# Where a split weight's remainder lies modulo 256 bytes: five wider buffers, each a pool of its own

## The chip, the cores and the metric

The kernel runs on one core of a Trainium2 chip. The metric is device time in microseconds (us) of one execution; lower is better. Three runs of the kernel before took 2660.53, 2660.72 and 2661.61 us, so its median is 2660.72 us. The engines are named as the profile names them: PE is the matrix engine (TensorE; PEld is its loading of weights), DVE is VectorE, ACT is ScalarE, POOL is GpSimd, SP is SyncE, which here issues most of the transfers.

## The reference

A decoder trunk of two layers over 256 positions of width 2048, all in float32:

```python
for i in range(DEPTH):                      # DEPTH = 2
    h = rms_norm(x, attn_norm[i])
    if i % 2 == 0:
        x = x + mla_mixer(h, ...)           # low-rank q and kv (rank 512), 16 heads, causal
    else:
        x = x + dilated_mixer(h, ...)       # 3 groups of windows (128,1), (512,4), (2048,16), 16 heads
    h = rms_norm(x, ffn_norm[i])
    x = x + conv_ffn(h, ...)                # up to 2 x 5632, causal convolution of width 3, silu gate, down
return rms_norm(x, final_norm)
```

Nearly all of the work is products of the 256 positions with weights that are read once: `dil_w_in` (2048 x 18432), `ffn_w_up` (2 x 2048 x 11264), `ffn_w_down` (2 x 5632 x 2048), the latent projections and the two output projections.

## The kernel before

**Split products.** Each float32 operand is split in two parts that PE multiplies in float32r form: a high part (`wh` of a weight, the first half of an activation tile) and the remainder (`wl`, the second half). ACT copies a piece of 1024 columns from the weights' ring `w` into `wh` (rounding it), DVE subtracts it from `w` and writes `wl`. A product is then high x high, high x low and low x high.

**Three ways to use a split weight.**
- A *unit* (`proj`, L142): the weight is the stationary operand and the activation `xs` or `a` the moving one. Matmuls with `wh` have 512 columns (high and low half of the activation together), those with `wl` 256 (the high half alone). All the wh matmuls of a unit come first and then all the wl ones, in the next unit the other way round (`runs`), so that up to 32 alike stand in a row. Projections of the dilated layer, up, down and output projections are units.
- *V* of the dilated layer (`load_tok2`, `proj_tok2`, L171 to L173): the activation is stationary, the weight moving, 512 columns. Three matmuls in turn: high with `wh`, low with `wh`, high with `wl`. V is done once for two pairs of heads and each of three groups, in four quarters.
- *Groups of seven products* in the feed-forward layers: four blocks of the up projection by Strassen's way, seven products in place of eight. `seven_ahead` (L957 to L959) uses sums of weights that were made earlier in HBM, `seven_here` (L1027 to L1029) makes them in SBUF for itself. The matmuls are of V's form: high with `wh`, low with `wh`, high with `wl`, weights moving. They are dealt out in portions of 6 or 12 matmuls between units (`slots`), after a unit's last matmul and with a wh run next.

The latent layer multiplies the normed latents `sqh` and `skvh` (256 columns, moving, or stationary for its V) with pieces of `wqb` and `wkvb` in `project` (through `mm3`, L109 to L111).

**Buffers.** Five buffers of 4096 bytes per partition for `wh` (pool `wsp`) and five for `wl` (pool `wspl`), each taken by whichever piece comes next as soon as one is free. Pools lie one behind the other. The residual stream, the activations `xs` and `a`, and `wh` all lie at one remainder modulo 256 bytes, since every pool between them takes a multiple of 256. Before `wspl` a tile `apart` of 64 bytes is put, so that all five `wl` buffers lie 64 bytes further, modulo 256. Behind them come `tab`, `work` (lo, sum and the like) and `small` (acc, sq, ms, rcol and small columns), also 64 bytes further, and then the weights' ring, where the remainder is that of `wh` again (the small pool is 192 bytes over a multiple of 256).

**Order.** Each engine runs its instructions in the order of the program. A unit first loads and splits its weights (`load`), then the matmuls follow, then a step or a portion of a group, then the evacuation of the unit before it. In the output projections (`out_proj`) and in the last down projection of a layer (`down` with `lastly`) two or three loads run ahead, and their products stop short of the last heads or blocks, which aren't ready; the rest of these products (`since`) follows later.

Of the kernel before, what the change touches and what calls it, by code (L numbers as in the profile page):

```python
# [18 lines left out]
F32 = mybir.dt.float32  # L19
# [14 lines left out]
RC = RANK // P  # L34
HEADS = 16
WS = 1024
NG = 3
GROUPS = ((128, 1), (512, 4), (2048, 16))
FFN = 5632
# [18 lines left out]
def trunk_kernel(tc, x_d, pos_d, gain_d, conv_d, const_d, mask_d, wqa_d, wkva_d, wqb_d, wkvb_d, wo_d,  # L58
                 win_d, dwo_d, wup_d, wdn_d, out_d):
    nc = tc.nc  # L60
    with ExitStack() as ctx:
# [1 line left out]
        resid = ctx.enter_context(tc.tile_pool(name="resid", bufs=1))  # L63
        wsp = ctx.enter_context(tc.tile_pool(name="wsp", bufs=5))
        act = ctx.enter_context(tc.tile_pool(name="act", bufs=16))
        apart = ctx.enter_context(tc.tile_pool(name="apart", bufs=1)).tile([P, 16], F32, name="apart", tag="apart")
        wspl = ctx.enter_context(tc.tile_pool(name="wspl", bufs=5))
        tab = ctx.enter_context(tc.tile_pool(name="tab", bufs=1))
        work = ctx.enter_context(tc.tile_pool(name="work", bufs=4))
        small = ctx.enter_context(tc.tile_pool(name="small", bufs=4))  # L70
# [5 lines left out]


        ring = {}

        def load(src, n, tok=0):  # L80

            some_ahead()
            wide = ring["wide"]
            w = []
            for a in range(0, n, wide):
                m = min(n - a, wide)
                t = ring["pool"].tile([P, wide], F32, name="w", tag="w")
                nc.sync.dma_start(t[:, :m], src[:, a:a + m])
                w += [t[:, c:c + min(m - c, WS)] for c in range(0, m, WS)]
            parts = []  # L90
            for i, w in enumerate(w):
                m = w.shape[-1]
                wh = wsp.tile([P, WS], F32R, name="wh", tag="wh")
                wl = wspl.tile([P, WS], F32R, name="wl", tag="wl")
                if i * WS < tok:
                    state["split"] = nc.scalar.activation(wh[:, :m], w, AF.Copy)  # L96
                    nc.vector.tensor_sub(wl[:, :m], w, wh[:, :m].bitcast(F32))  # L97
                else:
                    for h, t in enumerate((wh, wl)):
                        src2 = w[:, h * WS // 2:(h + 1) * WS // 2].rearrange("p (k c) -> p k c", c=T)  # L100
                        t4 = t.rearrange("p (k s c) -> p k s c", s=2, c=T)
                        nc.scalar.activation(t4[:, :, 0, :], src2, AF.Copy)
                        nc.vector.tensor_sub(t4[:, :, 1, :], src2, t4[:, :, 0, :].bitcast(F32))
                parts.append((wh, wl))
            return parts
# [40 lines left out]
        def load_tok2(srcs, q):  # L146


            some_ahead()
            w = ring["pool"].tile([P, D], F32, name="w", tag="w")  # L150
            for i, src in enumerate(srcs):
                nc.sync.dma_start(w[:, i * WS:(i + 1) * WS], src[q // 2][:, q % 2 * WS:(q % 2 + 1) * WS])
            w4 = w.rearrange("p (i k c) -> p i k c", i=2, c=T)
            parts = []
            for h in range(2):
                wh = wsp.tile([P, WS], F32R, name="wh", tag="wh")
                wl = wspl.tile([P, WS], F32R, name="wl", tag="wl")
                wh4, wl4 = (t.rearrange("p (k i c) -> p i k c", i=2, c=T) for t in (wh, wl))
                src = w4[:, :, 2 * h:2 * h + 2, :]
                nc.scalar.activation(wh4, src, AF.Copy)  # L160
                nc.vector.tensor_sub(wl4, src, wh4.bitcast(F32))  # L161
                parts += [(wh[:, ts(k, 512)], wl[:, ts(k, 512)]) for k in range(2)]
            return parts
# [138 lines left out]
        xs = [None] * KC  # L302
        dil_rope = []

        def squares(src, i, name, adder=nc.vector):
            if i == 0:
                acc = small.tile([P, T], F32, name="acc", tag="acc", bufs=2)
                state[name] = acc
                nc.scalar.activation(acc, src, AF.Square)
            else:  # L310
                sq = small.tile([P, T], F32, name="sq", tag="sq", bufs=1)
                nc.scalar.activation(sq, src, AF.Square)
                adder.tensor_add(state[name], state[name], sq)
# [41 lines left out]

        def rstd_x(paired=False, last=None):
            ps = sumsq("x", paired, last)
            ms = small.tile([P, 2], F32, name="ms", tag="ms", bufs=2)
            nc.vector.tensor_scalar(ms, ps, 1.0 / D, EPS, op0=ALU.mult, op1=ALU.add)
            r = small.tile([P, 2], F32, name="rcol", tag="rcol", bufs=2)  # L360
            nc.gpsimd.tensor_tensor(r, ms, negh, op=ALU.pow)
            return r

        def rstd_rank(name, rcol):

            ps = sumsq(name)
            r2 = small.tile([P, 2], F32, name="r2", tag="r2", bufs=1)
            nc.vector.tensor_mul(r2, rcol, rcol)
            ms = small.tile([P, 2], F32, name="ms", tag="ms", bufs=2)
            nc.vector.scalar_tensor_tensor(ms, ps, 1.0 / RANK, r2, op0=ALU.mult, op1=ALU.mult)  # L370
            nc.vector.tensor_scalar(ms, ms, EPS, None, op0=ALU.add)
            s = small.tile([P, 2], F32, name="s2", tag="s2", bufs=2)
            nc.gpsimd.tensor_tensor(s, ms, negh, op=ALU.pow)
            nc.vector.tensor_mul(s, s, rcol)
            return s
# [123 lines left out]
        def mla():  # L499
            mask = lat.tile([P, P + T], F32, name="mask")  # L500

            def keep_rank(name, b, res, ps):
                t = work.tile([P, T], F32, name="lo", tag="lo", bufs=2)
                nc.scalar.activation(t, ps[:, T:], AF.Copy)
                a = lat.tile([P, T], F32, name=f"rank{b}", tag=f"rank{b}")
                nc.vector.tensor_add(a, ps[:, :T], t)
                squares(a, b, name)
                res.append(a)

            st = {}  # L510
# [38 lines left out]
            for k in range(KC):  # L549
# [2 lines left out]
                if k % 4 == 0:  # L552
                    w = ring["pool"].tile([P, D], F32, name="w", tag="w")
                if k % 2 == 0:
                    wh = wsp.tile([P, WS], F32R, name="wh", tag="wh")
                    wl = wspl.tile([P, WS], F32R, name="wl", tag="wl")
                c = k % 2 * RANK
                if k % n == 0:
                    a = k % 4 * RANK
# [58 lines left out]


            def project(j):  # L620
                wq = load(wqb_d[j], 3 * RC * P, tok=D)
                wkv = load(wkvb_d[j], 4 * RC * P, tok=WS)
                h = {}

                def keep_q(e, ps):
# [225 lines left out]
        def ffn(layer, goff, ready):  # L851
# [9 lines left out]

            def col():
                rb["r"] = rstd_x()
                rb["n"] = small.tile([P, 2], F32, name="ms", tag="ms", bufs=2)
                nc.vector.tensor_scalar(rb["n"], rb["r"], -1.0, None, op0=ALU.mult)

            def wide():
# [44 lines left out]
            def seven_ahead(fb0):  # L912
# [6 lines left out]
                def product(i, q):  # L919
# [25 lines left out]
                        w4 = w4.rearrange("p f k c -> p k f c")  # L945
                        tiles += [w4[:, k:k + 2] for k in range(0, n, 2)]
                    for h, w5 in enumerate(tiles):
                        wh = wsp.tile([P, WS], F32R, name="wh", tag="wh")
                        wl = wspl.tile([P, WS], F32R, name="wl", tag="wl")
                        as4 = lambda t: t.rearrange("p (k f c) -> p k f c", k=2, f=4)  # L950
                        nc.scalar.activation(as4(wh), w5, AF.Copy)  # L951
                        nc.vector.tensor_sub(as4(wl), w5, as4(wh).bitcast(F32))  # L952
                        for k in range(2):
                            kk = 4 * q + 2 * h + k
                            xh, xl = stationary(name, kk)
                            bh, bl = wh[:, ts(k, HALF)], wl[:, ts(k, HALF)]
                            nc.tensor.matmul(ps[i], xh, bh, start=(kk == 0), stop=False)  # L957
                            nc.tensor.matmul(ps[i], xl, bh, start=False, stop=False)  # L958
                            nc.tensor.matmul(ps[i], xh, bl, start=False, stop=(kk == KC // 2 - 1))  # L959
# [58 lines left out]
            def seven_here(fb0):  # L1018
# [9 lines left out]
                    nc.tensor.matmul(ps[i], xl, wh, start=False, stop=False)  # L1028
                    nc.tensor.matmul(ps[i], xh, wl, start=False, stop=(kk == KC // 2 - 1))  # L1029

                def pair():
                    wh = wsp.tile([P, WS], F32R, name="wh", tag="wh")
                    wl = wspl.tile([P, WS], F32R, name="wl", tag="wl")
                    return wh, wl

                raw = {}

                def first(kk):
# [10 lines left out]
                    as4 = lambda t: t.rearrange("p (i f c) -> p i f c", i=2, f=4)  # L1049
                    t13 = fpool.tile([P, 2 * HALF], F32, name="t13", tag="t13")  # L1050
                    t24 = fpool.tile([P, 2 * HALF], F32, name="t24", tag="t24")
                    (bh, bl), (ch, cl) = pieces = [pair() for _ in range(2)]

                    nc.scalar.activation(as4(bh), w5[:, 0], AF.Copy)
                    nc.vector.tensor_add(as4(t13), w5[:, 1], w5[:, :, 0])
# [5 lines left out]

                def second(kk):
                    w5, t1, t4, t24 = raw[0]
                    dh, dl = pair()

                    nc.vector.tensor_add(t4[:, 0], w5[:, 1, 1], t1[:, 0])
                    nc.vector.tensor_add(t4[:, 1], t4[:, 0], w5[:, 0, 1])
                    nc.scalar.activation(dh, t24, AF.Copy)
                    nc.vector.tensor_sub(dl, t24, dh.bitcast(F32))
                    some([None, None, (dh, dl)], kk, (6, 4))  # L1070
# [22 lines left out]
                def third(q):  # L1093
# [7 lines left out]
                        nc.sync.dma_start(w5[:, f], src[1, 1, :, f, 4 * q:4 * q + 4])  # L1101
                    w5 = w.rearrange("p (f k c) -> p k f c", f=4, k=4)
                    for h in range(2):
                        bh, bl = pair()
                        as4 = lambda t: t.rearrange("p (k f c) -> p k f c", k=2, f=4)
                        nc.scalar.activation(as4(bh), w5[:, 2 * h:2 * h + 2], AF.Copy)
                        nc.vector.tensor_sub(as4(bl), w5[:, 2 * h:2 * h + 2], as4(bh).bitcast(F32))
# [273 lines left out]
```

## Time and profile before

| what | value |
|---|---|
| median of 3 runs | 2660.72 us |
| the profiled execution, its own time | 2661.63 us |
| its span | 2659.8 us |
| PE busy | 2646.2 us, 99% of the span |
| PEld busy | 2306.2 us, 87% |
| DVE busy | 2090.3 us, 79% |
| ACT busy | 1683.9 us, 63% |
| read from HBM, written | 656.69 MB, 119.54 MB |

How to read it: the profile is one execution. Busy is the time in which an engine has an instruction under way; matmuls overlap one another, so that the length of one (some 390 ns at 512 columns) is more than the distance to the next start. A row of a group reads: line, engine, operation, output from inputs, shapes, count, busy us, mean ns of one, idle time before. A row of the timeline reads: start in us from the span's start, length in us, engine, line, operation, how many alike are merged, and in brackets what ended the idle time before.

### The profile page before, as it was taken

What the parts mean: (1) busy time and instruction counts of PE and PEld (TensorE: products, weight loads), DVE (VectorE), ACT (ScalarE), POOL (GpSimd) and SP (SyncE); (2) the same over time, 40 slices, a digit from 0 to 9 for tenths busy, and PEclk for the clock granted to TensorE, in tenths of its full rate; (3) what the DMA queues carried; (4) which work ended last, traced back from release to release, by engine and by line L of the source; (5) the groups of instructions that cost most, each with busy time, mean ns of one, the idle gap of its engine ahead of it and who ended that gap; (6) DMA issues with size and microseconds to landing.
All of it is one profiled execution on the core that took longest, in us unless ns stands there. A gap on an engine that the chain in (4) does not pass through costs nothing.

```text
span 2659.8 us, 40506 instructions
## 1 busy us (share of the span) xinstructions
PE 2646.2 (99%) x14879; PEld 2306.2 (87%) x14879; DVE 2090.3 (79%) x3577; ACT 1683.9 (63%) x2661; POOL 215.7 (8%) x258
## 2 busy tenths in 40 slices
PE   9999999999999999999999999999999999999998
PEld 8998888888888888888888888888888888888887
DVE  8987989888888876677577667567688788789885
ACT  7775866676666674444455454455676777777776
POOL 2220000000000001112111212110000000000000
PEclk9999999999999999999999999999999999999999
DMA  7898775756766778999999999996457787897874
GB/s 262 241 239 275 236 253 176 236 184 211 239 194 234 226 254 262 317 280 280 322 272 286 312 286 295 292 272 190 177 184 241 237 268 250 270 300 249 262 240 143
DMA packets 310872, 661.45 MB, mean 249 GB/s; under 512 B 17808, under 2 KB 224016, under 8 KB 285456
## 3 DMA queue, kind: packets, MB, share of 16 engines
q1 hardware_dynamic: 231024, 541.22, 59.1%
q0 software_dynamic: 79360, 117.45, 21.1%
q8 instruction: 117, 1.92, 0.3%
q14 instruction: 83, 0.68, 0.1%
q10 hardware_dynamic: 288, 0.18, 0.0%
HBM read 656.69 MB, written 119.54 MB: 292 GB/s over the span
## 4 chain that ended last, share of the span: by engine, by line
PE 96%; DVE 2%; DMA 1%; ACT 1%; issue 0%; POOL 0%; DVEq 0%; ACTq 0%
PE pp L142 63%; PE ps L957 3%; PE ps L958 3%; PE ps L959 3%; PE pp L171 3%; PE pp L172 3%; PE pp L173 3%; PE pp L109 1%; PE pp L111 1%; PE pp L110 1%; PE pp L576 1%; DMA w<-in_wup 1%; DVE wl L97 1%; PE ps L1028 1%; PE ps L800 1%; PE po L837 1%
## 5 line engine op out<-in xcount | busy, mean ns | idle before, releaser
L97 DVE TENSOR_TENSOR wl<-w,wh 128x1024 fp32r<-128x1024 f32 x738 | 801.5, 1100 | 335.4 <-ACT wh L96 214.6
L96 ACT ACTIVATE wh<-w 128x1024 fp32r<-128x1024 f32 x738 | 702.4, 958 | 344.2 <-PE pp L142 199.3
L142 PE MATMUL pp<-xs,wh 128*128 128x512 f32 x3136 | 739.9, 390 | 0.0
L142 PEld LDWEIGHTS pp<-xs,wh 128*128 128x128 f32 x3136 | 581.9, 188 | 118.2 <-DVE xs L318 0.2
L142 PE MATMUL pp<-a,wh 128*128 128x512 f32 x1898 | 456.8, 391 | 0.5 <-ACT wh L96 0.5
L142 PEld LDWEIGHTS pp<-a,wh 128*128 128x128 f32 x1898 | 352.8, 188 | 74.1 <-ACT wh L96 0.7
L142 PE MATMUL pp<-xs,wl 128*128 128x256 f32 x3136 | 397.4, 282 | 0.0
L142 PEld LDWEIGHTS pp<-xs,wl 128*128 128x128 f32 x3136 | 389.0, 189 | 9.4
L952 DVE TENSOR_TENSOR wl<-w,wh 128x1024 fp32r<-128x1024 f32 x196 | 238.6, 1221 | 43.4 <-ACT wh L951 37.1
L951 ACT ACTIVATE wh<-w 128x1024 fp32r<-128x1024 f32 x196 | 206.9, 1057 | 73.6 <-PE ps L958 36.7
L142 PEld LDWEIGHTS pp<-a,wl 128*128 128x128 f32 x1898 | 242.5, 189 | 9.8
L142 PE MATMUL pp<-a,wl 128*128 128x256 f32 x1898 | 246.8, 281 | 0.0
L237 POOL DMA_DIRECT2D t<-in_wup x112 | 83.0, 748 | 1350.4 <-ACT wh L96 1286.8
L161 DVE TENSOR_TENSOR wl<-w,wh 128x1024 fp32r<-128x1024 f32 x96 | 116.2, 1217 | 63.4 <-ACT wh L160 51.5
L160 ACT ACTIVATE wh<-w 128x1024 fp32r<-128x1024 f32 x96 | 101.6, 1059 | 100.2 <-PE pp L172 46.0
L171 PE MATMUL pp<-wh,xs 128*128 128x512 f32 x384 | 151.9, 396 | 0.0
L173 PE MATMUL pp<-wl,xs 128*128 128x512 f32 x384 | 151.2, 394 | 0.0
L172 PE MATMUL pp<-wh,xs 128*128 128x512 f32 x384 | 151.1, 394 | 0.0
L265 ACT ACTIVATE lo<-pp 128x256 f32<-128x256 f32 x193 | 73.7, 382 | 104.4 <-PE pp L142 103.8
L125 ACT ACTIVATE pp<-x 128x512 f32<-128x512 f32 x142 | 84.4, 596 | 44.1 <-DVE x L425 41.8
L1136 DVE SCALAR_TENSOR_TENSOR cv<-upad,convs,cv 128x256 f32<-128x256 f32 x192 | 91.2, 480 | 8.7 <-ACT cv L1132 7.6
L173 PEld LDWEIGHTS pp<-wl,xs 128*128 128x128 f32 x384 | 72.0, 188 | 17.1
(349 smaller groups left out, 3728.1 us busy)
## 6 DMA issues: line engine op xcount, KB each, us to landing
w<-in_wup SPq DMA_DIRECT2D x200, 512.0 KB, 5.0
w<-in_win SPq DMA_DIRECT2D x96, 1024.0 KB, 7.6
t<-in_wup POOLq DMA_DIRECT2D x168, 512.0 KB, 9.8
w<-in_wup SPq DMA_DIRECT2D x56, 1024.0 KB, 4.8
w<-in_win SPq DMA_DIRECT2D x96, 512.0 KB, 7.6
w<-t SPq DMA_DIRECT2D x96, 512.0 KB, 4.8
w<-in_wdn SPq DMA_DIRECT2D x64, 704.0 KB, 5.7
w<-in_wdn SPq DMA_DIRECT2D x64, 512.0 KB, 5.0
```

What stands on the lines that cost most here:

```text
L96: state["split"] = nc.scalar.activation(wh[:, :m], w, AF.Copy)
L97: nc.vector.tensor_sub(wl[:, :m], w, wh[:, :m].bitcast(F32))
L125: nc.scalar.activation(dst, chunk.unsqueeze(1).to_broadcast([P, 2, 2, P]), AF.Copy, scale=0.5)
L142: nc.tensor.matmul(ps[:, i * T:], w_k, xs[k][:, :(2 - i) * T], start=(k == 0 and i == own), stop=(k == n - 1), skip_group_check=(i != own))
L160: nc.scalar.activation(wh4, src, AF.Copy)
L161: nc.vector.tensor_sub(wl4, src, wh4.bitcast(F32))
L171: nc.tensor.matmul(ps, xh, wh, start=k == 0, stop=False)
L172: nc.tensor.matmul(ps, xl, wh, start=False, stop=False)
L173: nc.tensor.matmul(ps, xh, wl, start=False, stop=k == KC - 1)
L951: nc.scalar.activation(as4(wh), w5, AF.Copy)
L952: nc.vector.tensor_sub(as4(wl), w5, as4(wh).bitcast(F32))
L1136: nc.vector.scalar_tensor_tensor(o, v, convs[:, cw + j:cw + j + 1], o, op0=ALU.mult, op1=ALU.add)
```

## The change

The five buffers of `wl` become five pools of one buffer each, 1024 + 48 floats (4288 bytes) wide. They are taken in strict turn. A piece uses 1024 floats of its buffer from a start that the caller chooses: with `apart=1` it lies 64 bytes further than `wh` modulo 256, with `apart=0` at the same remainder. Units and the first loop over `wqa` keep 64; V, the groups of seven products and the latent layer's `project` take 0. The tile `apart` goes. The buffers of `wl` take 896 bytes more in all; `small` gives 896 back: one buffer of `acc` less and two more of each of `ms` and `rcol` (they fall to the pool's count of four), and the sums of squares of the two latents move to the latent layer's own pool.

```diff
+WL = 5
+LINE = 16
...
-        apart = ctx.enter_context(tc.tile_pool(name="apart", bufs=1)).tile([P, 16], F32, name="apart", tag="apart")
-        wspl = ctx.enter_context(tc.tile_pool(name="wspl", bufs=5))
+        wspl = [ctx.enter_context(tc.tile_pool(name=f"wspl{i}", bufs=1)) for i in range(WL)]
...
+        turn_of = {"wl": 0}
+
+        def pair(apart):
+
+            wh = wsp.tile([P, WS], F32R, name="wh", tag="wh")
+            i = turn_of["wl"]
+            turn_of["wl"] = (i + 1) % WL
+            wl = wspl[i].tile([P, WS + 3 * LINE], F32R, name="wl", tag="wl")
+            o = (i + apart) % 4 * LINE
+            return wh, wl[:, o:o + WS]
+
+        def load(src, n, tok=0, apart=1):
...
-                wh = wsp.tile([P, WS], F32R, name="wh", tag="wh")
-                wl = wspl.tile([P, WS], F32R, name="wl", tag="wl")
+                wh, wl = pair(apart)
...
+                wh, wl = pair(0)
...
+                if pool is None:
+                    acc = small.tile([P, T], F32, name="acc", tag="acc", bufs=1)
+                else:
+                    acc = pool.tile([P, T], F32, name="acc" + name, tag="acc" + name)
...
-            ms = small.tile([P, 2], F32, name="ms", tag="ms", bufs=2)
+            ms = small.tile([P, 2], F32, name="ms", tag="ms")
...
+                    wh, wl = pair(1)
...
-                wq = load(wqb_d[j], 3 * RC * P, tok=D)
-                wkv = load(wkvb_d[j], 4 * RC * P, tok=WS)
+                wq = load(wqb_d[j], 3 * RC * P, tok=D, apart=0)
+                wkv = load(wkvb_d[j], 4 * RC * P, tok=WS, apart=0)
...
+                        wh, wl = pair(0)
+                    (bh, bl), (ch, cl) = pieces = [pair(0) for _ in range(2)]
+                    dh, dl = pair(0)
+                        bh, bl = pair(0)
```

More of the change, by code (lines that the diff above doesn't have):

```diff
@@ L78, in trunk_kernel @@
         ring = {}
-        def load(src, n, tok=0):
+        turn_of = {"wl": 0}
[7 more added lines that the diff above has]
+        def load(src, n, tok=0, apart=1):
             some_ahead()
@@ L155, in load_tok2 @@
             for h in range(2):
-                wh = wsp.tile([P, WS], F32R, name="wh", tag="wh")
-                wl = wspl.tile([P, WS], F32R, name="wl", tag="wl")
+                wh, wl = pair(0)
                 wh4, wl4 = (t.rearrange("p (k i c) -> p i k c", i=2, c=T) for t in (wh, wl))
@@ L303, in trunk_kernel, with squares @@
         dil_rope = []
-        def squares(src, i, name, adder=nc.vector):
+        def squares(src, i, name, adder=nc.vector, pool=None):
             if i == 0:
-                acc = small.tile([P, T], F32, name="acc", tag="acc", bufs=2)
+                if pool is None:
+                    acc = small.tile([P, T], F32, name="acc", tag="acc", bufs=1)
+                else:
+                    acc = pool.tile([P, T], F32, name="acc" + name, tag="acc" + name)
                 state[name] = acc
@@ L357, in rstd_x @@
             ps = sumsq("x", paired, last)
-            ms = small.tile([P, 2], F32, name="ms", tag="ms", bufs=2)
+            ms = small.tile([P, 2], F32, name="ms", tag="ms")
             nc.vector.tensor_scalar(ms, ps, 1.0 / D, EPS, op0=ALU.mult, op1=ALU.add)
-            r = small.tile([P, 2], F32, name="rcol", tag="rcol", bufs=2)
+            r = small.tile([P, 2], F32, name="rcol", tag="rcol")
             nc.gpsimd.tensor_tensor(r, ms, negh, op=ALU.pow)
@@ L368, in rstd_rank @@
             nc.vector.tensor_mul(r2, rcol, rcol)
-            ms = small.tile([P, 2], F32, name="ms", tag="ms", bufs=2)
+            ms = small.tile([P, 2], F32, name="ms", tag="ms")
             nc.vector.scalar_tensor_tensor(ms, ps, 1.0 / RANK, r2, op0=ALU.mult, op1=ALU.mult)
@@ L506, in keep_rank @@
                 nc.vector.tensor_add(a, ps[:, :T], t)
-                squares(a, b, name)
+                squares(a, b, name, pool=lat)
                 res.append(a)
@@ L554, in mla @@
                 if k % 2 == 0:
-                    wh = wsp.tile([P, WS], F32R, name="wh", tag="wh")
-                    wl = wspl.tile([P, WS], F32R, name="wl", tag="wl")
+                    wh, wl = pair(1)
                 c = k % 2 * RANK
@@ L863, in col @@
                 rb["r"] = rstd_x()
-                rb["n"] = small.tile([P, 2], F32, name="ms", tag="ms", bufs=2)
+                rb["n"] = small.tile([P, 2], F32, name="ms", tag="ms")
                 nc.vector.tensor_scalar(rb["n"], rb["r"], -1.0, None, op0=ALU.mult)
@@ L947, in product @@
                     for h, w5 in enumerate(tiles):
-                        wh = wsp.tile([P, WS], F32R, name="wh", tag="wh")
-                        wl = wspl.tile([P, WS], F32R, name="wl", tag="wl")
+                        wh, wl = pair(0)
                         as4 = lambda t: t.rearrange("p (k f c) -> p k f c", k=2, f=4)
@@ L1029, in product @@
                     nc.tensor.matmul(ps[i], xh, wl, start=False, stop=(kk == KC // 2 - 1))
[L1031 to L1034, printed above, removed]
                 raw = {}
@@ L1051, in first @@
                     t24 = fpool.tile([P, 2 * HALF], F32, name="t24", tag="t24")
-                    (bh, bl), (ch, cl) = pieces = [pair() for _ in range(2)]
+                    (bh, bl), (ch, cl) = pieces = [pair(0) for _ in range(2)]
                     nc.scalar.activation(as4(bh), w5[:, 0], AF.Copy)
@@ L1063, in second @@
                     w5, t1, t4, t24 = raw[0]
-                    dh, dl = pair()
+                    dh, dl = pair(0)
                     nc.vector.tensor_add(t4[:, 0], w5[:, 1, 1], t1[:, 0])
@@ L1103, in third @@
                     for h in range(2):
-                        bh, bl = pair()
+                        bh, bl = pair(0)
                         as4 = lambda t: t.rearrange("p (k f c) -> p k f c", k=2, f=4)
```

## The prediction

> **What bounds the kernel now.** I read the page first: its head, the busy times and the chain of work that ended last.
>
> ```profile
> span 2659.8 us, 40506 instructions
> PE 2646.2 (99%) x14879; PEld 2306.2 (87%) x14879; DVE 2090.3 (79%) x3577; ACT 1683.9 (63%) x2661; POOL 215.7 (8%) x258
> ...
> PE 96%; DVE 2%; DMA 1%; ACT 1%; issue 0%; POOL 0%; DVEq 0%; ACTq 0%
> ```
>
> TensorE (PE) is busy 99% of the span and holds 96% of the chain. Since a busy PE need not be one that works at its peak, the second view is the list of who waited for whom, on PE:
>
> ```profile
> PE pp L576 <- DVE xs L318: 1.4, 1, 1.4
> ...
> PE pp L142 <- ACT wh L96: 0.5, 1, 0.5
> PE pt L1029 <- DVE wl L1058: 0.4, 2, 0.2
> ```
>
> The longest entry is 1.4 us in total, and it lies in the first loop. So the time is the sum of the distances between the starts of successive matmuls, and whatever shortens these shortens the kernel, as long as no split becomes late. The third view is therefore the timeline of PE, start by start. (Its columns are start, length, engine, line; a row that ends in x6 merges six alike, and a row can reach back over the window's edge.) First a unit: 32 matmuls on pieces of wl, then a run on pieces of wh, then the first product of V:
>
> ```profile
> 1518.63 3.93 PE L142 MATMUL pp<-xs,wl 128*128 128x256 f32 x32
> 1522.40 1.55 PE L142 MATMUL pp<-xs,wh 128*128 128x512 f32 x6
> ...
> 1523.56 2.66 PE L142 MATMUL pp<-xs,wh 128*128 128x512 f32 x11
> 1526.05 0.39 PE L171 MATMUL pp<-wh,xs 128*128 128x512 f32 x1
> ```
>
> From 1522.40 to the sixth start at 1523.56 lie 5 distances of 232 ns; the other 11 take 2.49 us, 226 ns each. A 512-column matmul settles within about five starts. The 256-column ones of wl stand (3.93 - 0.28) / 31 = 118 ns apart. Now V, where wh and wl are the moving operand:
>
> ```profile
> 1499.78 0.40 PE L171 MATMUL pp<-wh,xs 128*128 128x512 f32 x1
> 1500.02 0.39 PE L172 MATMUL pp<-wh,xs 128*128 128x512 f32 x1
> 1500.24 0.39 PE L173 MATMUL pp<-wl,xs 128*128 128x512 f32 x1
> 1500.47 0.39 PE L171 MATMUL pp<-wh,xs 128*128 128x512 f32 x1
> 1500.69 0.40 PE L172 MATMUL pp<-wh,xs 128*128 128x512 f32 x1
> ...
> 1503.95 1.08 PE L142 MATMUL pp<-xs,wh 128*128 128x512 f32 x4
> 1504.64 3.11 PE L142 MATMUL pp<-xs,wh 128*128 128x512 f32 x13
> ```
>
> Eighteen distances fill 1503.95 - 1499.78 = 4.17 us: 231.7 ns each, and uneven (240, 220, 230, 220). They don't settle for as long as V lasts; the unit behind it does, after three starts of 230 ns: (3.11 - 0.39) / 12 = 226.7 ns. The groups of seven products look like V:
>
> ```profile
> 2172.52 0.39 PE L957 MATMUL ps<-wh,w 128*128 128x512 f32 x1
> ...
> 2176.47 0.39 PE L959 MATMUL ps<-wl,w 128*128 128x512 f32 x1
> 501.35 0.39 PE L1027 MATMUL ps<-wh,xs 128*128 128x512 f32 x1
> ...
> 504.13 2.21 PE L142 MATMUL pp<-a,wh 128*128 128x512 f32 x9
> ```
>
> That is 17 distances of 232.4 ns in the prepared groups and 12 of 231.7 ns in those formed on the spot. Same columns, same type, no wait: 226.7 in a unit, 232 in a group. What differs is addresses. In the long wh run of a unit, weights (wh) and moving operand (xs) have one remainder modulo 256 bytes throughout; in a wl run they differ by 64 throughout. In a group the moving operand jumps: wh, wh, wl, hence 0, 0, 64 against the weights that are loaded beside it. I read the uneven row as a settling that every third matmul starts anew. The dilated scores test this: they have the groups' order of products, but all operands at one remainder (qks lies in a pool at a multiple of 256 from wh).
>
> ```profile
> 1122.13 0.28 PE L109 MATMUL ps<-qks 128*128 128x256 f32 x1
> 1122.25 0.28 PE L110 MATMUL ps<-qks 128*128 128x256 f32 x1
> ...
> 1122.73 0.28 PE L111 MATMUL ps<-qks 128*128 128x256 f32 x1
> 1122.85 1.06 PE L800 MATMUL ps<-qk 128*128 128x128 f32 x8
> ```
>
> Six distances of exactly 120 ns, even from the first start. So the order of products doesn't make the unevenness, and a group whose wl stands at offset 0 should step like the 512-column run that has one remainder too, the unit's wh run: 226.7.
>
> The Trainium skill ("TensorE: Matmul & The Clock Gate", Part 2, step 1) speaks against the change: the moving operand and the weight load have separate SBUF read ports, so that a load takes no read bandwidth from the running matmul. By that alone no address matters, and the sum would be 0 instead of what follows. It doesn't explain 226.7 beside 232, so I give it only a rival's chance.
>
> **The change, part by part.** The groups' products are counted by a row of the page (L171, V) and, for L957 and then L1027, the whole span with the count of that line's matmuls; each count holds three times, for the line and its two neighbours:
>
> ```profile
> L171 PE MATMUL pp<-wh,xs 128*128 128x512 f32 x384 | 151.9, 396 | 0.0
> ...
> 0.00:2660.00 2660.00, 155.13 (x392) 73.75 (x392) 1.00 0.81 249
> 0.00:2660.00 2660.00, 66.15 (x168) 31.56 (x168) 1.00 0.81 249
> ```
>
> (1) *wl at offset 0 in V and the groups.* Steady step: V 3 x 384 x (231.7 - 226.7) = 5.8 us; prepared groups 3 x 392 x (232.4 - 226.7) = 6.7; groups on the spot 3 x 168 x (231.7 - 226.7) = 2.5; together 15.0 us off. Each stretch now has to settle after the wl run before it: 5 x (232 - 226.7) = 26.5 ns. By the code there are 54 stretches on the spot (24 of twelve, 24 of six, 6 thirds), some 72 prepared ones (98 quarters, partly two in a row) and some 18 of V: 144 x 26.5 ns = 3.8 us back. The unit run behind a stretch, now unsettled by 3 x 3.3 = 10 ns (1504.64 above; other stretches look up to twice that), starts settled: 144 x 15 ns = 2.2 us off. Net 13.4 us off. Bounds: 15.0 + 2.2 if the start costs nothing; the losing end is rival D.
>
> (2) *The splits that must keep up.* A split of 1024 columns feeds six products in a prepared group.
>
> ```profile
> L952 DVE TENSOR_TENSOR wl<-w,wh 128x1024 fp32r<-128x1024 f32 x196 | 238.6, 1221 | 43.4 <-ACT wh L951 37.1 <-PE pp L142 2.8 <-ACT wh L96 2.3
> ...
> 430.50:566.00 135.50, 135.50 (x731) 116.98 (x731) 114.86 (x151) 89.14 (x126) 0.57 (x1) 1.00 0.67 227
> ```
>
> VectorE needs 1.221 us where PE will take 6 x 226.7 = 1.36 us; around a group on the spot it is busy 114.9 of 135.5 us. With PE 2% faster there, cover remains; I cost it at 0. If it were gone, at most the 2.5 us of the groups on the spot are lost, wl at L1029 being late next. The operations that move to another remainder (lo, sum, acc, tables: from 64 to 192 beyond wh) don't feed the groups; 0.
>
> (3) *wq and wkv at offset 0.* Here sqh and skvh stand 32 bytes from wh, so that the offset stays uneven with 0 as with 64.
>
> ```profile
> 61.95 0.28 PE L109 MATMUL pp<-sqh,wl 128*128 128x256 f32 x1
> ...
> 63.71 0.28 PE L109 MATMUL pp<-sqh,wl 128*128 128x256 f32 x1
> ```
>
> 15 distances of 117.3 ns. Some 670 such products (8 pairs of heads, 60 for q and k and 24 for v) could go to the 120 of qks (+1.8 us) or to a distance 1 ns shorter (-0.7). I take +0.5, since the remainders will not be equal.
>
> (4) *Five pools of one buffer.* wl buffers are now taken in strict turn; before, whichever came free first. This differs only where loads run ahead of the last heads or blocks: at the start of the two output projections and at the end of the two down projections. The first of them:
>
> ```profile
> 183.32 1.22 DVE L97 TENSOR_TENSOR wl<-w,wh 128x1024 fp32r<-128x1024 f32 x1
> 184.88 0.42 DVE L405 TENSOR_TENSOR a<-po,a 128x256 fp32r<-128x256 f32 x1 [0.34 <-ACT a L404]
> ...
> 190.77 1.96 DVE L418 TENSOR_TENSOR x<-x,pp 128x256 f32<-128x256 f32 x5
> 190.15 0.64 PE L142 MATMUL pp<-a,wl 128*128 128x256 f32 x4
> ...
> 191.55 2.28 PE L142 MATMUL pp<-a,wl 128*128 128x256 f32 x18
> ```
>
> The split at 183.32 writes the first buffer of the fourth load. In strict turn it must take the second buffer of the first load, read last by the four wl products at 190.15. From about 190.5 it needs 1.22 us, while PE wants it after two of the eighteen products at 191.55: late by 0 to 0.3 us, or by up to 2.2 if the residual sums at 190.77 (1.96 us) stand before it; its neighbour is queued behind it. The other places have more room or one buffer like this. I take 1.0 us for all; bounds 0 and 5.
>
> (5) *acc in one buffer, those of the latents in their own pool, four of ms and rcol, no apart tile.* One sum of squares is read long before the next begins, and the bytes given and taken in front of the weights' ring cancel (896 more, 896 less), so w keeps its place: 0.
>
> Sum: -13.4 + 0.5 + 1.0 = -11.9 us. The profiled execution took 2661.6 us (span 2659.8), 0.9 over the median of 2660.7. So 2661.6 - 11.9 = 2649.7 for itself, and 2648.8 at the median: I say 2649.
>
> **The rivals.** *B, no address effect:* the groups step at 232 because each product there has new weights and a moving tile in use for three products. For it: V never settles. Against: the qks rows. Time: 2660.7 plus 1.5 of (3) and (4), 2662. *C, half:* every product is shortened only while wh follows wh, and the turn to wl still disturbs, because hi and lo halves of the weights alternate as well. Half of 15.0 off, no other term but 1.5: 2660.7 - 7.5 + 1.5 = 2655. Against: qks alternates likewise. *D, slower:* the offset of 64 spares the wl product a collision that wh has, as the 256-column runs suggest (118 at offset 64, 120 at 0). Then each of the 384 + 392 + 168 = 944 wl products goes to the dearest step in the row, 240 ns, 8 more than now: +7.6 + 1.5, 2670. It decides as soon as the mean step of a group exceeds 232. Against: the wh products at offset 0 average no more than the others do. That the buffers don't land where they should is excluded by arithmetic: a pool takes 1072 floats, 4288 bytes, and shifts its use by 64 (i + apart) modulo 256; 4288 i + 64 i = 17 x 256 i.
>
> **How the numbers follow.** Forecast 0.72, B 0.08, C 0.12, D 0.08. The forecast's own range: 2660.7 - 17.2 - 0.7 + 0 = 2643 to 2660.7 - 13.4 + 1.8 + 5 = 2654. The range 2645 to 2660 leaves out D, B and the forecast's outermost end, about 2 in 10. About 0.2%, 5.3 us, is what a measurement of this kernel can tell from no change. Faster by more: forecast and half of C, 0.78; within: the rest of C and B, 0.14; slower: 0.08.
>
> **What would show it.** Right: V rows 226.7 apart after five starts, near 4.08 us for eighteen; units unchanged at 226.7 and 118, and settled from the first start behind a group; qks at 120. Wrong: a group at 232 (B), still uneven but shorter (C), or above 232 (D); a wait of PE on wl of more than 2.5 us in the groups (2) or near 181 to 192 us (4); L109 above 120 ns apart (3).

## The result, and the profile after

| | median | runs | span of the profiled execution |
|---|---|---|---|
| before | 2661.16 us | 4, 2660.53 to 2662.01 | 2659.8 us |
| after | 2646.69 us | 4, 2646.49 to 2646.93 | 2645.1 us |

The ratio is 0.9945, with a 95% interval of 0.9928 to 0.9963: 14.5 us faster. The forecast was 2649.0 us, 11.7 us faster than the median it started from. The page of the kernel after, its head, its busy times and the first line of its chain:

```profile
span 2645.1 us, 40501 instructions
PE 2630.0 (99%) x14878; PEld 2304.8 (87%) x14879; DVE 2090.0 (79%) x3577; ACT 1683.4 (64%) x2661; POOL 216.4 (8%) x258
...
PE 97%; DVE 2%; DMA 1%; ACT 0%; issue 0%; POOL 0%; DVEq 0%; ACTq 0%; SPq 0%
```

TensorE is busy 16.2 us less (2646.2 before) with the same matmuls (one record is missing); the other engines' busy times are as they were. The list of who waited for whom, on PE, after:

```profile
PE pp L587 <- DVE xs L330: 2.6, 2, 1.7
...
PE pp L152 <- DVE wl L107: 0.4, 1, 0.4
...
PE pt L1039 <- DVE wl L1063: 0.2, 1, 0.2
```

There is still hardly any waiting, so the gain is again a matter of the distance between starts. The timeline of PE after (start, length, engine, line, operation), in V, in the unit that follows it, and in a prepared group:

```profile
1489.69 0.39 PE L182 MATMUL pp<-wl,xs 128*128 128x512 f32 x1
1489.92 0.39 PE L180 MATMUL pp<-wh,xs 128*128 128x512 f32 x1
1490.14 0.39 PE L181 MATMUL pp<-wh,xs 128*128 128x512 f32 x1
1490.37 0.39 PE L182 MATMUL pp<-wl,xs 128*128 128x512 f32 x1
...
1496.72 3.79 PE L152 MATMUL pp<-xs,wh 128*128 128x512 f32 x16
1500.34 3.93 PE L152 MATMUL pp<-xs,wl 128*128 128x256 f32 x32
...
2152.96 0.39 PE L967 MATMUL ps<-wh,w 128*128 128x512 f32 x1
2153.20 0.40 PE L968 MATMUL ps<-wh,w 128*128 128x512 f32 x1
2153.43 0.39 PE L969 MATMUL ps<-wl,w 128*128 128x512 f32 x1
2153.66 0.40 PE L967 MATMUL ps<-wh,w 128*128 128x512 f32 x1
...
2158.43 0.84 PE L152 MATMUL pp<-a,wh 128*128 128x512 f32 x3
```

From the start at 1489.69 to the unit's at 1496.72 lie 31 distances: 226.8 ns each, where 231.7 stood before, and the row is even (0.23, 0.22, 0.23). The unit behind V is settled from its first start, (3.79 - 0.39) / 15 = 226.7 ns, and its wl run keeps its step, (3.93 - 0.28) / 31 = 117.7 ns. The prepared group begins behind a wl run with 240, 230 and 230 ns and then settles; its 24 distances fill 5.47 us, 227.9 ns each.

Both executions start the same matmuls in the same order, so the distances can be summed line by line over the whole trace and subtracted:

| matmuls | count | before, us | after, us | difference |
|---|---|---|---|---|
| V | 1152 | 267.6 | 261.8 | -5.8 |
| prepared groups and groups on the spot | 1680 | 392.1 | 385.4 | -6.7 (-4.8 and -1.9) |
| units, wh (512 columns) | 5072 | 1158.2 | 1155.8 | -2.5 |
| units, wl (256 columns) | 5072 | 603.0 | 603.6 | +0.6 |
| latents' and scores' triples | 1008 | 122.9 | 122.7 | -0.2 |

The +0.6 of the wl row is one wait, in the first output projection. DVE and PE after, at that place:

```profile
190.40 0.41 DVE L430 TENSOR_TENSOR x<-x,pp 128x256 f32<-128x256 f32 x1
190.73 1.22 DVE L107 TENSOR_TENSOR wl<-w,wh 128x1024 fp32r<-128x1024 f32 x1
191.87 1.40 DVE L430 TENSOR_TENSOR x<-x,pp 128x256 f32<-128x256 f32 x4
...
191.18 0.40 PE L152 MATMUL pp<-a,wl 128*128 128x256 f32 x2
192.00 2.11 PE L152 MATMUL pp<-a,wl 128*128 128x256 f32 x16 [0.43 <-DVE wl L107]
```

The split at 190.73 stands behind one of the residual sums (190.40), ends at 191.95, and PE, which has done two of its eighteen wl matmuls, waits 0.43 us for it.

### The profile page after: what moved, and what is told of

It is laid out like the page before. It is cut to its first block, busy times and chain, and to the rows that moved or that the text cites. A ratio compares the mean times of both kernels' runs of the same rounds, so it can differ in the third digit from the quotient of the medians.

```text
span 2645.1 us, 40501 instructions
## 1 busy us (share of the span) xinstructions
PE 2630.0 (99%) x14878; PEld 2304.8 (87%) x14879; DVE 2090.0 (79%) x3577; ACT 1683.4 (64%) x2661; POOL 216.4 (8%) x258
## 4 chain that ended last, share of the span: by engine, by line
PE 97%; DVE 2%; DMA 1%; ACT 0%; issue 0%; POOL 0%; DVEq 0%; ACTq 0%; SPq 0%
PE pp L152 64%; PE ps L967 3%; PE ps L968 3%; PE ps L969 3%; PE pp L182 3%; PE pp L180 3%; PE pp L181 3%; PE pp L119 1%; PE pp L121 1%; PE pp L120 1%; PE pp L587 1%; PE ps L1038 1%; PE ps L1037 1%; PE ps L1039 1%; DVE wl L107 1%; PE po L848 1%
```

## The experiments

Each is an edit of the kernel after unless it says otherwise, and each ratio is to the kernel before, timed on the same chip. `pair(k)` and `apart=k` put wl 64 k bytes further than wh, modulo 256. Times "against the kernel after" that are given by groups of matmuls are sums of start distances, as in the table above; where nothing was changed, two traces differ in such sums by some tenths of a us, in the groups by 1.1 (the kernel before and experiment 1). A step is the distance between two starts, and a run has settled when its steps repeat.

**1. Everything of the change but the remainder.** All wl back at 64 (the first pair of lines below stands for V and every place of the groups): five pools in strict turn, the small tiles moved, and nothing else.

```diff
-                wh, wl = pair(0)
+                wh, wl = pair(1)
...
-                wq = load(wqb_d[j], 3 * RC * P, tok=D, apart=0)
-                wkv = load(wkvb_d[j], 4 * RC * P, tok=WS, apart=0)
+                wq = load(wqb_d[j], 3 * RC * P, tok=D, apart=1)
+                wkv = load(wkvb_d[j], 4 * RC * P, tok=WS, apart=1)
```

> The changed kernel with every piece of wl at 64, as before; the five pools in strict turn, the moved small tiles and the latents' own sums stay. Theory (the remainder alone makes the gain): V and the groups step at 232 again and the time is 2661.2 + 0.6 (the split that the strict turn delays) = 2661.8 us. Rival (the pools, or lo, sum and acc at another remainder, make it): it stays at 2646.7 us with groups at 226.7 ns.

Measured: 2661.37 us, ratio 1.0002 (0.9993 to 1.0011). V of this kernel, with wl at 64:

```profile
1497.06 0.39 PE L182 MATMUL pp<-wl,xs 128*128 128x512 f32 x1
1497.29 0.39 PE L180 MATMUL pp<-wh,xs 128*128 128x512 f32 x1
1497.52 0.40 PE L181 MATMUL pp<-wh,xs 128*128 128x512 f32 x1
1497.75 0.40 PE L182 MATMUL pp<-wl,xs 128*128 128x512 f32 x1
...
1502.86 3.80 PE L152 MATMUL pp<-xs,wh 128*128 128x512 f32 x16
```

25 distances in 5.80 us are 232.0 ns, as before the change; the sum over all V differs from the kernel before by less than 0.1 us. So the whole gain is that of the remainder, and rival B (no address effect) has fallen: the same program with other byte offsets takes 14.7 us more. The Trainium skill ("TensorE: Matmul & The Clock Gate", Part 2, step 1) has it that the streaming operand and the weight load read SBUF through ports of their own, so that a load takes no read bandwidth from the running matmul. If that were all, these two kernels would take the same time; for these float32r matmuls they don't, the addresses decide between 226.8 and 232.0 ns. What goes on at the ports no run here shows.

**2. Offset 0 for the units and the first loop as well.**

```diff
-        def load(src, n, tok=0, apart=1):
+        def load(src, n, tok=0, apart=0):
...
-                    wh, wl = pair(1)
+                    wh, wl = pair(0)
```

> The changed kernel with every piece of wl at 0, units too. Theory (a constant offset settles, and 0 settles at a step 2.3 ns dearer than 64): groups stay at 226.7 ns; the 5072 matmuls of wl in units go from 117.7 to 120 ns, +11.6 us; the wh runs behind them start settled, some 150 runs x 26 ns = -4 us: 2654 us. Rival (64 matters only where wl is the moving operand): units as they are, 2646.7 us.

Measured: 2656.35 us, ratio 0.9983 (0.9974 to 0.9993). A wl run of a unit in it, and the wh run behind:

```profile
212.74 4.00 PE L152 MATMUL pp<-a,wl 128*128 128x256 f32 x32
216.58 7.44 PE L152 MATMUL pp<-a,wh 128*128 128x512 f32 x32
```

(4.00 - 0.28) / 31 = 120.0 ns where the kernel after has 117.7. All wl matmuls of units take 9.0 us more than after; V and the groups keep their gain. So the 256-column matmuls of units do better at 64 than at 0, and those of 512 columns in V and the groups better at 0 than at 64: the two choices in the change are both needed. One half of the theory failed: the wh run behind doesn't start settled, its mean is (7.44 - 0.39) / 31 = 227.4 ns as in the kernel after, and the wh matmuls gain nothing (0.6 us more).

**3. The same jump, twice as far.** V and all places of the groups with wl at 128.

```diff
-                wh, wl = pair(0)
+                wh, wl = pair(2)
```

> The changed kernel with wl at 128 in V and in the groups, so that the moving operand jumps by 128 in place of 64. Theory (any jump unsettles): the steps in V stay uneven, mean between 229 and 236 ns, time 2653 to 2673 us. Rival (it is the distance of 64 that collides with the weights' load): V even at 226.7 ns, 2646.7 us.

Measured: 2660.77 us, ratio 1.0001 (0.9991 to 1.0010). V of this kernel:

```profile
1496.64 0.39 PE L180 MATMUL pp<-wh,xs 128*128 128x512 f32 x1
1496.87 0.39 PE L181 MATMUL pp<-wh,xs 128*128 128x512 f32 x1
1497.09 0.40 PE L182 MATMUL pp<-wl,xs 128*128 128x512 f32 x1
1497.33 0.39 PE L180 MATMUL pp<-wh,xs 128*128 128x512 f32 x1
...
1502.13 3.79 PE L152 MATMUL pp<-xs,wh 128*128 128x512 f32 x16
```

24 distances in 5.49 us are 228.7 ns, and they form a regular row: the product with wl as moving operand takes some 233 ns (1497.09 to 1497.33 by the rounded starts), the two with wh 226 to 227. Summed, V is 2.5 us below the kernel before, the groups 1.1 above it. The time came as a harmful jump has it, the shape did not: nothing starts anew here. This stretch is one of the 12 of V that stand behind a settled wh run. The six others, with the same addresses, have another row:

```profile
1231.79 0.39 PE L181 MATMUL pp<-wh,xs 128*128 128x512 f32 x1
...
1242.76 0.63 PE L152 MATMUL pp<-xs,wh 128*128 128x512 f32 x2
```

47 distances in 10.97 us are 233.4 ns; by the unrounded starts 230, 236 and 234 in turn, where the first row has 226, 227 and 234. The groups that start behind a wl run have the dearer row too, which is why they gain nothing over the kernel before and V does. So at a jump of 128 the addresses alone don't set the step: two regular rows are possible, and they go with what stands ahead. The irregular row of the kernel before belongs to the jump of 64.

**4. No jump, but not at offset 0.** wh and wl both at 64 against everything else, always (a pad of 64 bytes ahead of `wsp`, 192 + 64 behind it, wl pools of 4096 bytes and a pad of 640 behind them).

```diff
+        pads = [ctx.enter_context(tc.tile_pool(name="pad0", bufs=1)).tile([P, 16], F32, name="pad0", tag="pad0")]
         wsp = ctx.enter_context(tc.tile_pool(name="wsp", bufs=5))
+        ctx.enter_context(tc.tile_pool(name="pad1", bufs=1)).tile([P, 48], F32, name="pad1", tag="pad1")
...
+        ctx.enter_context(tc.tile_pool(name="pad2", bufs=1)).tile([P, 16], F32, name="pad2", tag="pad2")
...
+        ctx.enter_context(tc.tile_pool(name="pad3", bufs=1)).tile([P, 160], F32, name="pad3", tag="pad3")
...
-            wl = wspl[i].tile([P, WS + 3 * LINE], F32R, name="wl", tag="wl")
-            o = (i + apart) % 4 * LINE
-            return wh, wl[:, o:o + WS]
+            wl = wspl[i].tile([P, WS], F32R, name="wl", tag="wl")
+            return wh, wl
```

> wh and wl both at 64 in all uses (64 bytes in front of the wh buffers, 192 behind them), so that weights and activations stand at a constant offset of 64 everywhere. Theory (a constant offset settles, 64 cheaper than 0 by 2.3 ns as at 256 columns): the wh runs of units and the groups step evenly at 224.4 ns, the wl runs stay at 117.7: 2646.7 - (5072 + 2832) x 2.3 = 2629 us, and up to 4 us less since the wh runs start settled. Rival (only offset 0 settles a matmul of 512 columns): units' wh runs and the groups uneven at about 232 ns, 2646.7 + 7904 x 5 = 2686 us.

Measured: 2668.58 us, ratio 1.0031 (1.0019 to 1.0043). A wl run and the wh run behind it:

```profile
213.19 3.79 PE L155 MATMUL pp<-a,wl 128*128 128x256 f32 x32
216.82 7.62 PE L155 MATMUL pp<-a,wh 128*128 128x512 f32 x32
```

The 512-column row of the unit, at a constant offset of 64, has (7.62 - 0.39) / 31 = 233.2 ns (in some rows the starts alternate between 231 and 236, in others they stand evenly at 233), so it isn't constancy that settles a row at 226.7, but the offset 0. That is 27.1 us more over all wh matmuls of units than before. The moving operand of these matmuls stands where it stood, only the weights loaded beside it have moved, and the loads themselves are as long as in the kernel after (first row; the second is this run's):

```profile
L152 PEld LDWEIGHTS pp<-xs,wh 128*128 128x128 f32 x3136 | 581.9, 188 | 117.1 <-DVE xs L330 0.2
L155 PEld LDWEIGHTS pp<-xs,wh 128*128 128x128 f32 x3136 | 582.0, 188 | 133.2 <-DVE xs L333 0.2
```

So it isn't a longer load that PE waits for: where the weights lie changes the distance between the matmuls. In V and the groups, where the moving operand is the one that has moved, the same constant offset costs less: most of their stretches step at 229 ns on average and the others at 233, and they take 2.8 and 4.9 us less than in the kernel before (a jump of 64). This, with the wl row, is why the rival's 2686 us came out far too high although its account of the units holds. And a surprise in the other direction: this wl run steps (3.79 - 0.28) / 31 = 113.2 ns, not 117.7, though wl, xs and their offset are those of the kernel before; all wl matmuls of units together take 12.8 us less. Experiments 9 to 12 follow this up.

**5 to 8. Other offsets for the units' wl,** with V, the groups and the latents left at 0. Two of them keep steps of 64; two have steps of 32 (LINE is 8, buffers of 1024 + 56 floats, `ms`, `rcol` and `mx` with two buffers each to make room). The edit shown is that for 128; 192 has 3, and with LINE at 8 the steps 1 and 3 give 32 and 96. The first loop has the units' offset.

```diff
-        def load(src, n, tok=0, apart=1):
+        def load(src, n, tok=0, apart=2):
```

> The changed kernel with the units' wl at 128 in place of 64; groups, V and latents at 0 as they are. Theory (each offset has its own step, which the run before does not change): the step of the 5072 wl matmuls changes with the offset, at least 113.3 (the least seen with both at 64) and at most 121 ns (7 ns more for a jump of 128 at 512 columns suggests dear): 2646.7 + 5.07 x (s - 117.7), from 2625 to 2663 us, dear more likely. Rival (the run before decides: behind an even wh run the wl run always steps at 117.7): 2646.7 us.

> The changed kernel with the units' wl at 192, that is 64 on the other side of the activations. Theory (each offset has its own step): another step than 117.7, between 113.3 and 121 ns, 2625 to 2663 us; with the sign of no account it would be 117.7 again, 2646.7 us. Rival (the run before decides): 117.7 and 2646.7 us.

> The changed kernel with the units' wl at 32 (buffers 32 bytes wider, given back by fewer buffers of ms, rcol and mx); groups, V and latents at 0. Theory (each offset has its own step): the latent products at 32 stand 113 to 121 ns apart, 117 on average, so about 117 and uneven: 2643 to 2650 us. Rival (only multiples of 64 count): 32 is as good as 0, 120 ns, 2656 us as with every piece at 0.

> The changed kernel with the units' wl at 96. Theory (each offset has its own step): between the steps of 64 (117.7) and 128, 2625 to 2663 us. Rival (only multiples of 64 count): as 64, 2646.7 us.

The steps are those of one wl run near 213 us and the wh run behind it, each from a row as above (the kernel after has 3.93 us for 32 wl matmuls and 7.44 for the 32 wh behind them):

| units' wl at | median, us | ratio to before | wl step, ns | wh behind it, mean ns |
|---|---|---|---|---|
| 0 (experiment 2) | 2656.35 | 0.9983 (0.9974 to 0.9993) | 120.0 | 227.4 |
| 32 | 2652.40 | 0.9968 (0.9955 to 0.9980) | 118.4 | 228.4 |
| 64 (after) | 2646.69 | 0.9945 (0.9928 to 0.9963) | 117.7 | 227.4 |
| 96 | 2646.18 | 0.9947 (0.9932 to 0.9962) | 117.4 | 227.0 |
| 128 | 2658.56 | 0.9993 (0.9984 to 1.0002) | 120.3 | 227.7 |
| 192 | 2651.44 | 0.9968 (0.9956 to 0.9979) | 117.7 | 228.1 |

The timelines of the kernels with 128, with 192 and with 96, in this order:

```profile
212.87 4.01 PE L152 MATMUL pp<-a,wl 128*128 128x256 f32 x32
```

```profile
216.02 7.46 PE L152 MATMUL pp<-a,wh 128*128 128x512 f32 x32
```

```profile
213.23 3.92 PE L152 MATMUL pp<-a,wl 128*128 128x256 f32 x32
216.98 7.20 PE L152 MATMUL pp<-a,wh 128*128 128x512 f32 x31
```

At 128 the wl matmuls themselves are dearer, (4.01 - 0.28) / 31 = 120.3 ns, 11.3 us in all against the kernel after. At 192 they are as good as at 64, but the wh run behind has (7.46 - 0.39) / 31 = 228.1 ns: it needs about ten starts to settle rather than five, and wh takes 2.7 us more in all. The groups behind wl runs start in the same way and take 2.5 us more. At 96 the wh run settles after one start, (7.20 - 0.39) / 30 = 227.0 ns. Offsets of 64 and 96 can't be told apart in time. So an offset has two prices, its own step and what it leaves to the next run. Of the theories, 128 came out dear as forecast, and against the rival of that run, since its wl runs stand behind even wh runs too. At 192 and 96 the step is within 0.3 ns of that at 64, where another was forecast for 192. At 32 it is 118.4, neither that of 0 nor that of 64, so the rival that only multiples of 64 count has fallen; the time is 2.4 us above the range that was given.

**9 to 12. What decides between 113.3 and 117.7 ns.** In the trace of experiment 4 the step of a wl run follows from the matmuls just ahead of it: behind a wh row that ends 231, 236, or evenly at 233, it is 113, behind one that ends 236, 231 it is 118. In the kernel after, by the starts in its trace, 270 of 277 wl runs of ten or more step at 118. Three experiments disturb the turn of a unit from wh to wl, at 249 places (248 in the swap), in three ways; the addresses stay. In the first the last wh matmul is issued as two of 256 columns, in the second the last wh and the first wl matmul change places, in the third the first wl matmul is issued as two of 128. The edit of the swap:

```diff
-            for i in order:
-                for k in ks:
-                    w_k = w[k * P // WS][i][:, k * P % WS:k * P % WS + P]
-                    nc.tensor.matmul(ps[:, i * T:], w_k, xs[k][:, :(2 - i) * T], start=(k == 0 and i == own),
-                                     stop=(k == n - 1), skip_group_check=(i != own))
+            def one(i, k, a, b):
+                w_k = w[k * P // WS][i][:, k * P % WS:k * P % WS + P]
+                nc.tensor.matmul(ps[:, i * T + a:i * T + b], w_k, xs[k][:, a:b], start=(k == 0 and i == own),
+                                 stop=(k == n - 1 and b == (2 - i) * T), skip_group_check=(i != own))
+
+            todo = [(i, k) for i in order for k in ks]
+            if order[0] == 0 and len(ks) > 1:
+                j = len(ks)
+                todo[j - 1], todo[j] = todo[j], todo[j - 1]
+            for i, k in todo:
+                one(i, k, 0, (2 - i) * T)
```

> The changed kernel, and at each turn of a unit from wh to wl the last wh matmul is issued as two of 256 columns (high half, then low half). Theory (two steps are open to a wl run with the same addresses, 117.7 and 113.3 ns, and what comes just before it decides): a turn that no longer follows an even 226.7 ns row lets the wl runs fall to 113.3 more often; if all of them do, 5034 x 4.4 ns = 22 us off and some 150 turns x 13 ns = 2 us on: 2627 us. Rival (the 113.3 ns step needs the uneven 231/236 ns row of the run with both at 64, and nothing short of it): wl runs stay at 117.7, and the time is 2646.7 + 2 = 2648.7 us.

> The changed kernel, and at each turn of a unit from wh to wl the last wh and the first wl matmul change places. Theory (what comes just before a wl run decides its step): wl runs fall to 113.3 ns more often, 2625 us if all do. Rival: they stay at 117.7 ns, 2646 to 2648 us.

> The changed kernel, and at each turn of a unit from wh to wl the first wl matmul is issued as two of 128 columns. Theory (what comes just before a wl run decides its step): wl runs fall to 113.3 ns more often, 2625 us if all do. Rival: they stay at 117.7 ns; two of 128 columns cost at most as much again as one of 256, so 2646 to 2649 us.

Measured: halves 2652.95 us, ratio 0.9970 (0.9958 to 0.9982); swap 2632.45 us, 0.9893 (0.9876 to 0.9909); quarters 2670.66 us, 1.0038 (1.0023 to 1.0053). The timeline of the swap, and below it a wl run of the halves:

```profile
210.80 0.84 PE L151 MATMUL pp<-a,wh 128*128 128x512 f32 x3
211.48 0.28 PE L151 MATMUL pp<-a,wl 128*128 128x256 f32 x1
211.60 0.40 PE L151 MATMUL pp<-a,wh 128*128 128x512 f32 x1
211.83 3.68 PE L151 MATMUL pp<-a,wl 128*128 128x256 f32 x31
215.35 7.21 PE L151 MATMUL pp<-a,wh 128*128 128x512 f32 x31
```

```profile
211.89 3.93 PE L151 MATMUL pp<-a,wl 128*128 128x256 f32 x32
```

With the swap, the wl run steps (3.68 - 0.28) / 30 = 113.3 ns, exactly half of the 226.7 of 512 columns; with the halves it stays at 117.7. By the starts, 242 of 276 wl runs of the swapped kernel have the shorter step; 29 of the 34 others follow no wh run of a unit, so that no swap stands ahead of them. The wl matmuls take 17.5 us less than in the kernel after, wh 1.8 and the groups 1.2 more: 14.4 of the 22 us that all runs would bring. Of the halves, the rival's account holds for the step; their 6 us over the kernel after are 2.0 of wh and 4.2 of the groups, 2.6 of them waits for wl splits in those on the spot.

The quarters bring wl runs to 113 ns as well, but their first seven distances, 58, 113, 167, 119, 120, 119 and 118 ns, cost more than the rest gains (wl +12.9 us against after). The other half of their loss lies in the groups, +11.0 us. Of this kernel, the list of waits, one window of the busy times (the granted clock is the third figure from the end) and the timeline:

```profile
PE ps L1047 <- DVE wl L1070: 7.4, 6, 4.0
```

```profile
656.00:660.50 4.50, 3.83 (x9) 3.06 (x10) 4.50 (x6) 3.60 (x6) 0.00 (x0) 0.50 0.52 164
```

```profile
652.29 0.40 PE L1046 MATMUL ps<-wh,xs 128*128 128x512 f32 x1
656.67 0.79 PE L1047 MATMUL ps<-wl,xs 128*128 128x512 f32 x1 [3.98 <-DVE wl L1070]
657.26 0.63 PE L1045 MATMUL ps<-wh,xs 128*128 128x512 f32 x1
657.69 0.63 PE L1046 MATMUL ps<-wh,xs 128*128 128x512 f32 x1
```

In a group on the spot PE waits 3.98 us for a split, and the granted clock behind it is 0.50: the matmuls that follow are 430 ns apart (657.26 to 657.69). The Trainium skill ("TensorE: Matmul & The Clock Gate", Part 1) says that an idle stretch of about 3.4 us throttles the clock to half; this trace agrees, with 3.98 us of idling and 0.50. Why the splits came late there was not followed up.

Last, the swap with all wl at offset 0 (experiment 2 with the swap):

> wl at offset 0 everywhere, units too (2656.35 us without the swap, wl runs of units at 120.3 ns), and at each turn of a unit from wh to wl the last wh and the first wl matmul change places. Theory (113.3 ns, half of a settled 512-column step of 226.7, is open to a wl run at offset 0 as well, and the swap enters it): 5034 x 7 ns = 35 us off, 2621 us. Rival (at offset 0 a wl run knows only its 120 ns step, and the units' offset of 64 is what makes 113.3 possible): 2655 to 2658 us.

Measured: 2659.39 us, ratio 0.9997 (0.9987 to 1.0006). A wl run in the timeline of this kernel:

```profile
212.58 3.88 PE L151 MATMUL pp<-a,wl 128*128 128x256 f32 x31
```

(3.88 - 0.28) / 30 = 120.0 ns: the rival was right. At offset 0 a wl run has one step only, whatever stands ahead; at 64 it has two, and the short one must be entered. The swap on the kernel after, 2632.45 us, is the fastest of all these, and 14 us below the kernel after.

## Why the prediction was right

**Step 1, wl at offset 0 in V and the groups: right.** The settled step became 226.7 to 226.8 ns as forecast, and experiment 1 shows that the remainder alone brings it. Of the 15.0 us, V's 5.8 came whole and the groups' 9.2 as 6.7 (5.6 against experiment 1, so this is good to about 1 us). The lost 2.5 are starts, forecast at 3.8. The start behind a wl run was sized well: the median over the trace after is 231, 236, 228, 233, 231 and then 227, 25 ns above five settled ones. But it is paid 112 times, 61 in prepared groups and 51 on the spot; of the 18 stretches of V, 12 stand behind a settled wh run and pay nothing. The units behind the stretches gained 2.5 us (2.2 forecast).

**The reading behind it was only half right.** "A settling that every third matmul starts anew" and "one remainder settles" gave the right number, because the change goes to offset 0. Experiment 4 shows that a constant remainder of 64 leaves 512 columns at 233 ns, and experiment 3 that a jump of 128 makes a regular row. The forecast took its 226.7 ns from a run at offset 0, so the number didn't hang on the wider reading; for a change to another constant offset that reading would have misled. What the runs support is narrower: 226.7 ns is the settled step of a 512-column matmul at offset 0 to the weights loaded beside it, and every other offset that was tried costs more: 6.5 ns at a constant 64 in units, 2 to 7 at a constant 64 in V and the groups, 2 or 7 over the three products at a jump of 128 (by what stands ahead), 5 at a jump of 64. Two things stay open. The offsets are those of the kernel's layout, and no run moves both operands together away from their usual remainder, so whether the difference counts or the place of each isn't separated. And why the hardware does so no run here shows.

**Step 2, the splits keep up (0): right for the change.** PE waits 0.2 us for a split in the groups on the spot. The bound of 2.5 us was too tight as a statement of what can happen there: with other timing ahead, as in the halves and the quarters, the same place lost 2.6 and 7.4 us to waits, and more behind them.

**Step 3, the latents' weights (+0.5): nothing.** Their step is what it was:

```profile
61.72 0.28 PE L119 MATMUL pp<-sqh,wl 128*128 128x256 f32 x1
...
63.48 0.28 PE L119 MATMUL pp<-sqh,wl 128*128 128x256 f32 x1
```

15 distances in 1.76 us, 117.3 ns.

**Step 4, strict turn (+1.0): +0.6,** one wait, at the place named and by the mechanism named (a residual sum ahead of the split), 0.43 us by the profile's list and 0.6 by the distance.

**Step 5: 0,** and experiment 1, which has it whole, agrees within its interval.

Together: the starts cost 1.3 us less than forecast, the units behind gained 0.3 more, the latents lost nothing (0.5) and the turn 0.4 less: 2.5 us of the 2.6 between 11.9 forecast and 14.5 measured. With the groups' sum good to 1 us only, so close a match is partly luck.

**The rivals.** B fell with experiment 1. C, half the effect, fell with the even row of V. D's premise, that 64 is cheaper than 0, holds for 256 columns (experiment 2: 120.0 at 0, 117.7 at 64); carrying it over to 512 would have been the mistake, and whether a collision is behind it no run shows. What follows from the separate read ports of the Trainium skill ("TensorE: Matmul & The Clock Gate", Part 2, step 1), that no address matters, was given a rival's chance and didn't hold for these matmuls.

## What to carry to other kernels

When PE never waits and matmuls of one form have two different steps in one trace, compare the addresses of the operands before anything else, by form: here 512 columns were fastest with the moving operand and the weights beside it at one remainder modulo 256 bytes, and 256 columns, of the offsets tried, with 64 or 96 between them. Judge an offset by its own step and by how many starts the next run needs to settle. And when one run of alike matmuls shows two settled steps with the same addresses, look at the two or three matmuls ahead of it: exchanging two of them was worth as much as the whole change of addresses.

## What was not expected

- With the same addresses a run of 256-column matmuls has two settled steps, 113.3 and 117.7 ns, and stays for up to 32 matmuls in the one that it entered. An even 226.7 ns row ahead of it leads to 117.7; one wl matmul put ahead of the last wh leads to 113.3.
- At offset 0 the same matmuls step at 120.0 ns, with the swap or without it.
- At a constant offset of 64, rows of 512 columns in units alternate between 231 and 236 ns or stand at 233, over all 32 matmuls; they never reach 226.7.
- The products of V and the groups at a jump of 128 have two rows with the same addresses as well, 228.8 and 233.3 ns on average. At offset 0 they settle at one, 226.7.
